# A hybrid decoder layer on one core: each head's first step issued with the output of the head in front, four heads' keys turned by blocks, and lags set per head

## The chip, the cores and the metric

The kernel runs on one core of a Trainium2 chip. The metric is device time in microseconds (us) of one execution; smaller is better. The median of three runs is given, with their lowest and highest.

## What is computed

One layer of a decoder on x of 1024 positions by 1024 channels, all in float32: a token mixer and an MLP, each behind an RMS norm and with a residual, and a last RMS norm.

```python
h = rms_norm(x, norm_mix_g)
u = h @ w_in                                   # 256 pool channels, then q, f, i, g of 6 heads x 128
y_pool = pool_mixer(u_pool, pool_w, pool_scale)
y_hgrn = hgrn2_mixer(q_raw, f_raw, i_raw, g_raw, lb, hgrn_norm_g)
x = x + concat(y_pool, y_hgrn) @ w_out
h2 = rms_norm(x, norm_mlp_g)
x = x + square(relu(h2 @ w_up)) @ w_down       # 4096 wide
return rms_norm(x, final_norm_g)
```

The pool mixer takes means over the last 2, 4, 8 and 16 positions minus the position itself, then a small linear map. Each of the six HGRN heads is a gated linear recurrence with a 128 by 128 state:

```python
S_t = diag(f_t) * S_{t-1} + (1 - f_t) i_t^T    # f = lb + (1 - lb) * sigmoid(z)
o_t = S_t^T q_t
```

followed by an RMS norm per head and a swish gate. It may be computed in chunks of positions: scores within a chunk, and a state handed from chunk to chunk.

## The kernel before

**Dense work.** A dense product in float32 is split in two parts, hi and lo, and made of three matmuls (`mm3`, L129: hi·hi at L132, hi·lo at L133, lo·hi at L134). One such triple is a *step* here. The MLP is dense work alone and the change doesn't touch it.

**Heads.** `hgrn(hd)` (L417) is a generator that makes one head's recurrence out of six stages. Between two stages it stops, and dense work goes on. What stands before a stop is the preparation of the stage that the stop names; what stands behind it are the stage's matmuls, and what follows from them:

- up to "near": the products d0 and d1 and the first `deepen` (three multiplies that work decays into q and k) on VectorE (DVE), and copies `kq` on ScalarE (ACT), L434 and L435;
- "near": column sums (L415) and small matmuls (L443) of neighbouring positions into one bank of PSUM, `sc_near`, which DVE takes into the scores (`take`, L463 and L451); then `deepen` for 2, 4 and 8, with `kq` copies for 4, 8 and 16;
- "middle": matmuls for 4, 8 and 16 into a bank `sc_middle`, taken by DVE as well; `deepen` for 16 and 32;
- "far": scores over 32 and 64 positions; `deepen` for 64;
- "keys": the keys are transposed. Heads 0, 1, 4 and 5 do it on the matmul engine (PE) as `ptk` (L520). Heads 2 and 3 do it *by blocks*: DVE transposes blocks of 32 (L157) and DMAs on SyncE's queue (SP) write them out (L164) and fetch them back in order (L167);
- "updates": what each chunk adds to the state, `pu`: 14 matmuls (L530), or 56 smaller ones (L533) when the keys came by blocks; DVE then adds the states up (`st`);
- "output": the output matmuls `po` (L550, L552), squares on ACT (L555), the reciprocal root on GpSimd (POOL, L141), the scaled output `on` on DVE (L557), and, except for the last head, its transpose by blocks and DMAs.

**What lies beside a head.** `beside(hd)` (L651) gives dense work while head hd runs: q and f of the next head, then a gate. Head 4 has the first pool tile there (`pool_input(0)`). Head 5 has gate 4, then `pool_output(0)`, which is two psp groups of three matmuls (L634), then `pool_input(1)`, 12 steps of gate 5, `pool_output(1)` and the rest. `pool_input` goes from dense matmuls `ps_pool` to `u` (L376), the windowed sums `win` on DVE (L614 to L620), and their split: `whi_win` on ACT (L126), `wlo_win` on DVE (L127). The matmul at psp takes these two.

**What sets the order.** The loop at L770 writes out PE's order by hand: before each stage of head hd it takes so many steps of dense work as `LAGS` says, then goes on with the head's generator. DVE, ACT, POOL and SP get an order from a scheduler, which the tiles' dependences and PE's order shape; each engine then runs its own list in order. `score_ps` has two banks in rotation, used by near, middle, both far ones and by psp; `misc_ps` has three, `dense_ps` three. The decays of a head, `dec`, have a single buffer, as have `Kn` and `S`.

Of the kernel before, what the change touches and what calls it, by code (L numbers as in the profile page):

```python
# [10 lines left out]
F32 = mybir.dt.float32  # L11
# [6 lines left out]
P = 128  # L18
S = 1024
D = 1024  # L20
NT = S // P
# [3 lines left out]
NH = 6  # L25
# [5 lines left out]


STAGES = ("near", "middle", "far", "keys", "updates", "output")
LAGS = {48: (5, 14, 8, 4, 1, 9), 64: (6, 19, 10, 0, 16, 10), 96: (6, 19, 10, 0, 18, 14)}
LAGS = {steps: dict(zip(STAGES, lags)) for steps, lags in LAGS.items()}
FIRST_LAG = 9
WARM_UP = 8
MIX_ORDER = (2, 3, 4, 5, 6, 0, 1, 7)
# [2 lines left out]
TRIO = 3  # L41
# [24 lines left out]
def kernel(  # L66
# [23 lines left out]
    small = ctx.enter_context(tc.tile_pool(name="small", bufs=4))  # L90
# [106 lines left out]
    def mix_tile(n, name):  # L197

        return mixp.tile([P, S], F32, tag="mix" if n < NH - 2 else "late", name=name, bufs=NH - 2 if n < NH - 2 else 2)
# [4 lines left out]
    with ExitStack() as pa:  # L204
# [21 lines left out]
        def queries(t, m):  # L226

            return strided(t, m, [(HALF - m, 2), (2 * m, HALF // (2 * m)), (1, m)])

        def keys(t, m):  # L230
            return strided(t, 0, [(HALF + m, 2), (2 * m, HALF // (2 * m)), (1, m)])

        def sibling(t, of_keys, m):

            n = HALF // m
            off, step = (1, n - 1) if of_keys else (0, n + 1)
            return strided(t, off, [(step, 2), (2, n // 2), (0, m)])
# [28 lines left out]
        vts = {}  # L266
# [63 lines left out]
        def finish(work):  # L330

            while True:
                try:
                    next(work)
                except StopIteration as end:
                    return end.value
# [80 lines left out]
        def hgrn(hd, q, f, k, vt):  # L417
# [10 lines left out]
            dec = ha.tile([P, S], F32, tag="T", name=f"dec_{hd}", bufs=1)  # L428
            t_m, off = deepen(q, k, f, dec, 0, 1)
# [39 lines left out]
            for m in (4, 8, 16):  # L469
                t_m, off = deepen(q, k, t_m, dec, off, m // 2)  # L470
# [10 lines left out]
            t_m, off = deepen(q, k, t_m, dec, off, 16)  # L481
            kq = pairs_of(32)
            t_m, off = deepen(q, k, t_m, dec, off, 32)
# [16 lines left out]
                )  # L500
            act.copy(sc[:64, :4, 64:], ps[:64, :256].rearrange("p (c t) -> p c t", c=4))
            act.copy(sc[64:, 4:, :64], ps[64:, 256:].rearrange("p (c t) -> p c t", c=4))
            t_m, off = deepen(q, k, t_m, dec, off, 64)

            kn = ha.tile([P, NT, P], F32, tag="Kn", name=f"kn_{hd}", bufs=1)
            st = ha.tile([P, NT, P], F32, tag="S", name=f"st_{hd}", bufs=1)
            yield "keys"


            by_blocks = hd in (TRIO - 1, TRIO)  # L510
            if by_blocks:
                turned = ha.tile([P, 4, NT - 1, B], F32, tag="pair", name=f"turned_k_{hd}", bufs=3)
                blocks_turned(turned, k[:, :(NT - 1) * P].rearrange("p (c t) -> p c t", t=P))
# [55 lines left out]
        def deepen(q, k, t_m, dec, off, m):  # L569


            n = S // (2 * m)
            dve.tensor_tensor(out=queries(q, m), in0=queries(q, m), in1=sibling(t_m, False, m), op=ALU.mult)
            dve.tensor_tensor(out=keys(k, m), in0=keys(k, m), in1=sibling(t_m, True, m), op=ALU.mult)
            tv = t_m.rearrange("p (n two) -> p n two", two=2)
            nxt = dec[:, off:off + n]
            dve.tensor_tensor(out=nxt, in0=tv[:, :, 0], in1=tv[:, :, 1], op=ALU.mult)
            return nxt, off + n

        def mixed(hd, on, gate, place=misc_ps):  # L580
            t = mix_tile(hd, f"mix_{2 + hd}")
            mix[2 + hd] = t
            if hd < NH - 1:
                by_quarter = "p (c a i) -> p a c i"
                dve.tensor_tensor(
                    out=t.rearrange(by_quarter, a=4, i=B), in0=on.rearrange("p a (c i) -> p a c i", i=B),
                    in1=gate.rearrange(by_quarter, a=4, i=B), op=ALU.mult,
                )
                return
            for b in range(2):  # L590
                pt = place(f"pto_{hd}_{b}")
                for c in range(4):
                    pe.transpose(pt[:, c * P:(c + 1) * P], on[:, 4 * b + c, :], ident)
                sl = slice(b * 512, (b + 1) * 512)
                dve.tensor_tensor(out=t[:, sl], in0=pt, in1=gate[:, sl], op=ALU.mult)
# [55 lines left out]
        def beside(hd):  # L651

            if hd == TRIO:
                yield from gate(hd - 1)
            if hd + 1 < NH:
                heads[hd + 1] = q, f, k = head_tiles(hd + 1)
                wq = ready_w.pop("q", None) or q_weights(hd + 1)
                for h in range(2):
                    yield from gated(q, wq, h, f"q_{hd + 1}")
                wf = ready_w.pop("f", None) or f_weights(hd + 1)  # L660
                for h in range(2):
                    yield from forget(f, k, wf, h, hd + 1)
            if hd == TRIO - 1:
                yield from dense_V(1)
            elif hd + 2 < NH:
                yield from gate(hd)
            elif hd + 1 < NH:
                pooled[0] = yield from pool_input(0, [mix_tile(NH - 1, f"win{n}_0") for n in range(2)])
            else:
                wins = [ha.tile([P, S], F32, tag=tag, name=f"win{tag}_1", bufs=n) for tag, n in (("K", 2), ("F", 1))]  # L670
                yield from gate(hd - 1)
                pool_output(0, pooled[0])
                pooled[1] = yield from pool_input(1, wins)
                work = gate(hd)
                for _ in range(KT + KT // 2):
                    yield next(work)
                pool_output(1, pooled[1])
                yield from work

        heads, gates, pooled, ready_w, xts, w0 = {}, {}, {}, {}, {}, []  # L680
# [11 lines left out]
        with tc.manual_schedule(engines={mybir.EngineType.PE, mybir.EngineType.DVE, mybir.EngineType.Activation}):  # L692
# [68 lines left out]
            for n in range(2):  # L761
                for e in range(2):
                    nc.sync.dma_start(pw[e * 64:(e + 1) * 64, n, :], pool_w[0, 2 * n + e])
            chain = hgrn(0, *heads[0], vts[0])
            stage = next(chain)
        for e in range(2):
# [3 lines left out]
        with tc.manual_schedule(engines={mybir.EngineType.PE}):  # L770
            for hd in range(NH):
                work = beside(hd)
                lags = LAGS[{TRIO - 1: 96, TRIO: 64}.get(hd, 48)]
                if hd:
                    chain = hgrn(hd, *heads[hd], vts[hd])
                    stage = next(chain)
                while stage:
                    for _ in range(lags[stage] + (FIRST_LAG if hd == 0 and stage == "near" else 0)):
                        next(work, None)
                    if stage == "middle" and hd:  # L780
                        mixed(hd - 1, on, gates[hd - 1])
                    try:
                        stage = next(chain)
                    except StopIteration as end:
                        on, stage = end.value, None
                finish(work)

        def row_block(src, r0, n, c0, name):
# [597 lines left out]
```

## Time and profile before

| | |
|---|---|
| Time, median of three runs | 1065.08 us (1065.07 to 1065.22) |
| Time of the profiled execution | 1065.75 us |
| Its span, first to last instruction | 1063.9 us |
| Mean granted TensorE clock | 0.999 |
| Matmuls on PE | 5960 |
| Instructions in all | 14749 |

The profile is of one execution. What the profiled execution took beyond its span, 1.85 us, lies before the first and after the last instruction. A row of a timeline has the start in the span, the duration, engine, line, operation, output and inputs, and how many instructions went into it; durations of neighbouring rows overlap, since instructions are pipelined, so a cost is the distance from start to start. "128*32" is the part of the array that a matmul uses. A bracket at a row's end is idle time of the engine before it, and what ended it. Lines of the changed kernel are 5 to 8 higher than before's.

### The profile page before, as it was taken

The page shows a single profiled execution, that of the slowest core. Times are in us where ns is not written, and L with a number is a line of the kernel's source. Part 1 is how long each engine was busy: PE and PEld are TensorE (multiplying, and loading weights), DVE is VectorE, ACT ScalarE, POOL GpSimd, SP SyncE. Part 2 cuts the span into 40 slices and gives each one's busy share as a digit, 9 for nine tenths or more (in the row PEclk, how much of TensorE's full clock was granted, in tenths as well). Part 3 has the DMA queues.
Part 4 walks back from the last instruction along what each step waited for, and adds up shares of the span by engine and source line. Part 5 has one row for each costly group of instructions (what it writes and reads, how often), then busy time and mean ns, then how long its engine had stood idle before and what let it go on. Part 6 is the DMA issues. An engine that isn't in the chain of part 4 may idle for free.

```text
span 1063.9 us, 14749 instructions
## 1 busy us (share of the span) xinstructions
PE 1055.2 (99%) x5960; PEld 883.6 (83%) x5960; DVE 750.2 (71%) x934; ACT 444.8 (42%) x716; POOL 77.3 (7%) x126
## 2 busy tenths in 40 slices
PE   9999999999999999999999999999999999999997
PEld 8988888988888888888888888888888888888886
DVE  5377685366688824898855865786979877777775
ACT  5856544344544622563223223322434332424234
POOL 0001010001000111101101100100100000000001
PEclk9999999999999999999999999999999999999999
DMA  9521122132211633135434433528983344253104
GB/s 308 177 61 47 64 71 75 46 96 74 60 41 41 233 135 102 66 102 195 179 100 175 178 118 140 189 108 323 387 318 119 119 160 180 96 209 148 40 1 159
DMA packets 75557, 144.67 MB, mean 136 GB/s; under 512 B 5600, under 2 KB 48352, under 8 KB 71904
## 3 DMA queue, kind: packets, MB, share of 16 engines
q1 hardware_dynamic: 64848, 108.16, 30.0%
q0 software_dynamic: 9344, 33.56, 8.1%
q10 hardware_dynamic: 1296, 2.00, 0.5%
q8 instruction: 47, 0.77, 0.3%
q14 instruction: 22, 0.18, 0.1%
HBM read 102.41 MB, written 41.29 MB: 135 GB/s over the span
## 4 chain that ended last, share of the span: by engine, by line
PE 96%; DVE 2%; issue 1%; DMA 1%; POOL 0%; SPq 0%; ACT 0%; POOLq 0%
PE ps_ua L134 5%; PE ps_ua L133 5%; PE ps_ua L132 5%; PE ps_dx L132 5%; PE ps_dx L133 5%; PE ps_dx L134 5%; PE ps_v L304 3%; PE ps_dy L132 3%; PE ps_uc L134 3%; PE ps_dy L133 3%; PE ps_uc L133 3%; PE ps_dy L134 3%; PE ps_uc L132 3%; PE ps_o L134 3%; PE ps_o L133 3%; PE ps_o L132 2%
## 5 line engine op out<-in xcount | busy, mean ns | idle before, releaser
L126 ACT CAST wdop<-raw_wd 128x2048 fp32r<-128x2048 f32 x28 | 53.6, 1913 | 154.9 <-PE ps_dy L134 49.9
L132 PE MATMUL ps_ua<-h2op,whi_wu 128*128 128x512 f32 x256 | 99.7, 389 | 0.0
L134 PE MATMUL ps_ua<-h2op,wlo_wu 128*128 128x512 f32 x256 | 99.6, 389 | 0.0
L133 PE MATMUL ps_ua<-h2op,whi_wu 128*128 128x512 f32 x256 | 99.6, 389 | 0.0
L132 PE MATMUL ps_dx<-wdop,hop 128*128 128x512 f32 x252 | 98.0, 389 | 0.0
L133 PE MATMUL ps_dx<-wdop,hop 128*128 128x512 f32 x252 | 98.0, 389 | 0.0
L134 PE MATMUL ps_dx<-wdop,hop 128*128 128x512 f32 x252 | 98.0, 389 | 0.0
L127 DVE TENSOR_TENSOR wdop<-raw_wd,wdop 128x2048 fp32r<-128x2048 f32 x28 | 64.1, 2289 | 28.3 <-ACT wdop L126 28.3
L126 ACT CAST hop<-hraw 128x2048 fp32r<-128x2048 f32 x28 | 53.4, 1910 | 32.8 <-DMA hraw<-hid 20.7
L127 DVE TENSOR_TENSOR hop<-hraw,hop 128x2048 fp32r<-128x2048 f32 x28 | 63.9, 2283 | 2.6 <-ACT hop L126 2.6
L126 ACT CAST whi_wu<-wsum 128x1024 fp32r<-128x1024 f32 x22 | 23.2, 1054 | 94.4 <-DVE wsum L845 34.8
L127 DVE TENSOR_TENSOR wlo_wu<-raw_wu,whi_wu 128x1024 fp32r<-128x1024 f32 x23 | 28.0, 1221 | 47.0 <-ACT whi_wu L126 47.0
L848 DVE TENSOR_TENSOR x<-ps_dx,x 128x512 f32<-128x512 f32 x64 | 43.9, 687 | 18.7 <-PE ps_dx L134 18.7
L133 PEld LDWEIGHTS ps_ua<-h2op,whi_wu 128*128 128x128 f32 x256 | 48.1, 188 | 10.0
L132 PEld LDWEIGHTS ps_ua<-h2op,whi_wu 128*128 128x128 f32 x256 | 48.0, 188 | 10.0
L134 PEld LDWEIGHTS ps_ua<-h2op,wlo_wu 128*128 128x128 f32 x256 | 48.0, 188 | 9.9
L134 PEld LDWEIGHTS ps_dx<-wdop,hop 128*128 128x128 f32 x252 | 47.3, 188 | 9.9
L132 PEld LDWEIGHTS ps_dx<-wdop,hop 128*128 128x128 f32 x252 | 47.3, 188 | 9.8
L133 PEld LDWEIGHTS ps_dx<-wdop,hop 128*128 128x128 f32 x252 | 47.3, 188 | 9.7
L1081 POOL DMA_DIRECT2D hid<-hid x56 | 29.8, 532 | 283.6 <-DVE hid L1078 216.5
L132 PE MATMUL ps_uc<-h2op,whi_wu 128*128 128x512 f32 x128 | 49.8, 389 | 0.0
L133 PE MATMUL ps_uc<-h2op,whi_wu 128*128 128x512 f32 x128 | 49.8, 389 | 0.0
(290 smaller groups left out, 2699.3 us busy)
## 6 DMA issues: line engine op xcount, KB each, us to landing
hid<-hid POOLq DMA_DIRECT2D x56, 512.0 KB, 3.2
hraw<-hid SPq DMA_DIRECT2D x28, 1024.0 KB, 5.0
raw_wu<-in_w_up_dram SPq DMA_DIRECT2D x32, 512.0 KB, 3.8
raw_wd<-in_w_down_dram SPq DMA_DIRECT2D x16, 1024.0 KB, 7.1
xt<-in_x_t_dram SPq DMA_DIRECT2D x16, 256.0 KB, 5.6
xn<-in_x_dram SPq DMA_DIRECT2D x8, 512.0 KB, 7.4
x<-x_mid SPq DMA_DIRECT2D x8, 512.0 KB, 5.6
raw_q<-in_w_in_dram SPq DMA_DIRECT2D x6, 512.0 KB, 4.0
```

The source lines that it names most:

```text
L126: act.copy(hi, src)
L127: dve.tensor_tensor(out=lo, in0=src, in1=hi.bitcast(F32), op=ALU.subtract)
L132: pe.matmul(ps, lh, rh, start=start, stop=False, skip_group_check=goes_on)
L133: pe.matmul(ps, lh, rl, start=False, stop=False, skip_group_check=goes_on)
L134: pe.matmul(ps, ll, rh, start=False, stop=stop, skip_group_check=goes_on)
L304: pe.matmul(banks[i][:, :VC], hT[h][part][:, j, i * P:(i + 1) * P], w[:, b, :], start=j == 0 and part == 0 and w is wh, stop=j == KT - 1 a ...
L848: dve.tensor_tensor(out=out_, in0=a, in1=b, op=ALU.add)
L1081: nc.gpsimd.dma_start(store[n][:, at, :], t)
```

## The change

Five things change.

1. `LAGS` is given for each head, instead of for three kinds of heads (by how much dense work there is).
2. Heads 1 to 4 turn their keys by blocks (`TURNED_KEYS`), instead of 2 and 3.
3. The last `deepen`, for 64, writes its decays to a tile of its own, `chunks`, with two buffers, and no longer to the head's `dec`.
4. At the stage "output" of a head, the next head's generator is made and run up to its first stop ahead of the output; behind the output its near stage is issued at once, before the rest of the dense work. Lags for near are 0 from head 1 on.
5. The multiply of a head's output with its gate (`mixed`) is issued before the next head's "far", not before its "middle".

```diff
-LAGS = {48: (5, 14, 8, 4, 1, 9), 64: (6, 19, 10, 0, 16, 10), 96: (6, 19, 10, 0, 18, 14)}
-LAGS = {steps: dict(zip(STAGES, lags)) for steps, lags in LAGS.items()}
+LAGS = (
+    (5, 14, 8, 4, 1, 9), (0, 14, 8, 0, 16, 9), (0, 19, 10, 0, 18, 14), (0, 12, 10, 0, 20, 17), (0, 11, 8, 0, 16, 10),
+    (0, 11, 8, 4, 1, 9),
+)
+LAGS = [dict(zip(STAGES, lags)) for lags in LAGS]
+
+TURNED_KEYS = range(1, NH - 1)
...
-            t_m, off = deepen(q, k, t_m, dec, off, 64)
+            chunks = small.tile([P, NT], F32, tag="chunks", name=f"chunks_{hd}", bufs=2)
+            t_m, _ = deepen(q, k, t_m, chunks, 0, 64)
...
-            by_blocks = hd in (TRIO - 1, TRIO)
+            by_blocks = hd in TURNED_KEYS
...
-                lags = LAGS[{TRIO - 1: 96, TRIO: 64}.get(hd, 48)]
-                if hd:
-                    chain = hgrn(hd, *heads[hd], vts[hd])
-                    stage = next(chain)
+                lags, then = LAGS[hd], None
                 while stage:
                     for _ in range(lags[stage] + (FIRST_LAG if hd == 0 and stage == "near" else 0)):
                         next(work, None)
-                    if stage == "middle" and hd:
+                    if stage == "far" and hd:
                         mixed(hd - 1, on, gates[hd - 1])
+                    if stage == "output" and hd + 1 < NH:
+                        then = hgrn(hd + 1, *heads[hd + 1], vts[hd + 1])
+                        next(then)
                     try:
                         stage = next(chain)
                     except StopIteration as end:
                         on, stage = end.value, None
+                chain = then
+                stage = next(chain) if chain else None
                 finish(work)
```

Three places show what moves. The first is PE at head 5's near matmuls. In before they stand inside the dense work of gate 4 (`ps_g`); L415 and L443 write `sc_near`:

```order
L133 MATMUL ps_g_0_3108<-hT_lo_138,whi_g_2975 128x512
L134 MATMUL ps_g_0_3108<-hT_hi_137,wlo_g_2976 128x512
L415 MATMUL sc_near<-d_5_3092,ones 32x256 x4
L415 MATMUL sc_near<-d_5_3095,ones 32x128 x4
L443 MATMUL sc_near<-kq_2_3102 32x2x16 [waits Activation_49]
L443 MATMUL sc_near<-kq_2_3102 32x2x16 x15
L132 MATMUL ps_g_0_3108<-hT_hi_137,whi_g_2975 128x512
```

In the changed kernel they stand right behind head 4's last output matmuls, `po_1`:

```order
L556 MATMUL po_1_3094<-V_1860,scores 128x128
L558 MATMUL po_1_3094<-st_2909,Q_2356 128x128 [waits DVE_49]
L420 MATMUL sc_near<-d_5_3062,ones 32x256 x4
L420 MATMUL sc_near<-d_5_3065,ones 32x128 x4
L448 MATMUL sc_near<-kq_2_3072 32x2x16 [waits Activation_49]
L448 MATMUL sc_near<-kq_2_3072 32x2x16 x15
L137 MATMUL ps_pool_1_3046<-hT_hi_139,whi_pool_2973 128x512
L138 MATMUL ps_pool_1_3046<-hT_lo_140,whi_pool_2973 128x512
```

So near moved from behind the first pool tile's steps and some steps of gate to the place before the last three steps of the pool tile.

The second place is PE at the two psp groups of `pool_output(0)`, with the gate's last matmul ahead. Before, with the first `sc_middle` of head 5 farther behind:

```order
L134 MATMUL ps_g_1_3181<-hT_hi_139,wlo_g_2976 128x512
L132 MATMUL psp_0_3210<-whi_win_3086,pw_hi 128x512 [waits Activation_49]
L133 MATMUL psp_0_3210<-wlo_win_3087,pw_hi 128x512 [waits DVE_49]
L134 MATMUL psp_0_3210<-whi_win_3086,pw_lo 128x512
L132 MATMUL psp_1_3216<-whi_win_3086,pw_hi 128x512 [waits DVE_49,PE_49,Activation_49]
...
L134 MATMUL ps_pool_0_3235<-hT_hi_137,wlo_pool_3226 128x512 [waits DVE_49]
...
L443 MATMUL sc_middle<-kq_4_3154 32x2x16 [waits PE_49,Activation_49]
```

In the changed kernel `sc_middle` stands ahead, 15 dense matmuls before psp:

```order
L448 MATMUL sc_middle<-kq_4_3152 32x2x16 [waits Activation_49]
...
L139 MATMUL ps_g_1_3222<-hT_hi_139,wlo_g_2980 128x512
L137 MATMUL psp_0_3316<-whi_win_3185,pw_hi 128x512 [waits PE_49,Activation_49]
L138 MATMUL psp_0_3316<-wlo_win_3186,pw_hi 128x512 [waits DVE_49]
L139 MATMUL psp_0_3316<-whi_win_3185,pw_lo 128x512
L137 MATMUL psp_1_3322<-whi_win_3185,pw_hi 128x512 [waits DVE_49,PE_49,Activation_49]
...
L139 MATMUL ps_pool_0_3341<-hT_hi_137,wlo_pool_3332 128x512 [waits DVE_49]
```

The order of banks in `score_ps` is now near, middle, psp, psp, where it was near, psp, psp, middle.

The third place is DVE around the windowed sums `win`: from head 4's last `on` (L557) to the split of the second pool tile's weights, `wlo_pool`. In before the sums follow `u`, with nothing of head 5 between:

```order
L557 TENSOR_TENSOR on_3009<-po_1_3028,rstd_o_1_3044 128x512 [waits Pool_49]
L157 STREAM_TRANSPOSE turned_3047<-on_3009 128x1024 [waits DVE_49,PE_49]
L376 TENSOR_TENSOR u_2966<-ps_pool_1_3005,rms_row 128x4x128 [waits PE_49]
L614 TENSOR_TENSOR win_0_2964<-u_2966 128x1023 [waits DVE_49]
...
L463 COPY_PREDICATED within<-dmask,sc_near 128x256 [waits PE_49]
L573 TENSOR_TENSOR Q_2665<-Q_2665,dec_3097 128x2x64x4 [waits Activation_49]
L127 TENSOR_TENSOR wlo_win_3087<-win_0_2964,whi_win_3086 128x512 [waits Activation_49] x2
...
L127 TENSOR_TENSOR wlo_pool_3226<-raw_pool_3223,whi_pool_3225 128x1024 [waits DMAHW6_49]
```

In the changed kernel, the stretch from the second `on` to the first sum:

```order
L563 TENSOR_TENSOR on_3075<-po_1_3094,rstd_o_1_3110 128x512 [waits Pool_49]
L456 COPY_PREDICATED within<-lmask,sc_near 128x2x32x2 [waits DVE_49]
L162 STREAM_TRANSPOSE turned_3113<-on_3075 128x1024 [waits DVE_49]
L579 TENSOR_TENSOR Q_2732<-Q_2732,dec_3067 128x2x32x8 [waits Activation_49]
L580 TENSOR_TENSOR K_2734<-K_2734,dec_3067 128x2x32x8 [waits Activation_49]
L381 TENSOR_TENSOR u_2970<-ps_pool_1_3046,rms_row 128x4x128 [waits PE_49]
L579 TENSOR_TENSOR Q_2732<-Q_2732,dec_3067 128x2x16x16 [waits Activation_49]
L620 TENSOR_TENSOR win_0_2968<-u_2970 128x1023 [waits DVE_49]
L580 TENSOR_TENSOR K_2734<-K_2734,dec_3067 128x2x16x16 [waits Activation_49]
```

And the one behind the sums, up to `wlo_pool`:

```order
L626 SCALAR_TENSOR_TENSOR win_0_2968<-win_0_2969,pconst,u_2970 64x1024 [waits DVE_49]
L456 COPY_PREDICATED within<-lmask,sc_middle 128x2x16x4 [waits PE_49]
L381 TENSOR_TENSOR g_3193<-ps_g_0_3194,rms_row 128x512 [waits DVE_49]
L132 TENSOR_TENSOR wlo_win_3186<-win_0_2968,whi_win_3185 128x512 [waits Activation_49] x2
L391 SCALAR_TENSOR_TENSOR g_3193<-ps_g_0_3194,hg,g_3193 128x512 [waits Activation_49]
L456 COPY_PREDICATED within<-lmask,sc_middle 128x2x8x8
L579 TENSOR_TENSOR Q_2732<-Q_2732,dec_3067 128x2x8x32
L456 COPY_PREDICATED within<-lmask,sc_middle 128x2x4x16 [waits DVE_49]
L580 TENSOR_TENSOR K_2734<-K_2734,dec_3067 128x2x8x32
L381 TENSOR_TENSOR g_3193<-ps_g_1_3222,rms_row 128x512 [waits PE_49]
L132 TENSOR_TENSOR wlo_pool_3332<-raw_pool_3329,whi_pool_3331 128x1024 [waits Activation_49]
```

With that, four multiplies of head 5's `deepen` and the last take of near stand ahead of the split of `win`, which stood beside or behind it before, and the three takes of `sc_middle` stand among it, ahead of `wlo_pool`.

## The prediction

> **What bounds the kernel now.** I read the page first: its busy shares, then the chain that ended last.
>
> ```profile
> PE 1055.2 (99%) x5960; PEld 883.6 (83%) x5960; DVE 750.2 (71%) x934; ACT 444.8 (42%) x716; POOL 77.3 (7%) x126
> ...
> PEclk9999999999999999999999999999999999999999
> ...
> PE 96%; DVE 2%; issue 1%; DMA 1%; POOL 0%; SPq 0%; ACT 0%; POOLq 0%
> ```
>
> The matmul engine, PE, is busy for 1055.2 of the span's 1063.9 us, and the chain runs along it for 96%. The next view is the list of waits on PE, two rows in all:
>
> ```profile
> PE warm L251 <- DVE junk L249: 1.2, 1, 1.2
> PE ps_v L304 <- DVE wlo_v L127: 0.6, 1, 0.6
> ```
>
> Both lie at the kernel's start. From there on PE never waits for VectorE (DVE), so two things alone can move the time: fewer or shorter PE instructions, and new waits. The kernel's spare time is in the distance between an operand's end and the matmul that takes it, which a busy share doesn't show; for that I read the timelines of PE and DVE side by side at each place where the change moves a matmul nearer to its operand.
>
> **What the change takes from PE.** The timeline of PE around head 1's key transposes:
>
> ```profile
> 129.84 0.93 PE L520 MATMUL ptk<-ident,K 128*128 128x128 f32 x7
> 130.52 0.48 PE L132 MATMUL ps_f<-hT_hi,whi_f 128*128 128x512 f32 x1
> 130.84 0.40 PE L133 MATMUL ps_f<-hT_lo,whi_f 128*128 128x512 f32 x1
> 131.07 0.40 PE L134 MATMUL ps_f<-hT_hi,wlo_f 128*128 128x512 f32 x1
> 131.31 1.72 PE L530 MATMUL pu<-V,kn 128*128 128x128 f32 x14
> 132.78 0.48 PE L132 MATMUL ps_g<-hT_hi,whi_g 128*128 128x512 f32 x1
> ```
>
> Columns: start, duration, engine, line, operation, count. Durations overlap; what counts is start to start. The seven transposes take 0.68 (130.52 − 129.84). The first dense matmul behind them takes 0.32 to the next, where later ones take 0.23 (131.07 − 130.84): a return from small matmuls to dense ones costs 0.09. Heads 1 and 4 lose one such group each: 2 × (0.68 + 0.09) = 1.54 us gained.
>
> Their updates are then made by blocks, as head 2's are now:
>
> ```profile
> 184.00 1.74 PE L533 MATMUL pu<-V,kn 128*32 128x128 f32 x56
> 185.66 0.44 PE L132 MATMUL ps_v<-whi_v,hT_hi 128*128 128x384 f32 x1
> ```
>
> 56 small matmuls take 1.66 where the 14 large ones above took 1.47 (132.78 − 131.31): 2 × 0.19 = 0.38 us lost.
>
> The near matmuls of heads 1 to 5 now stand right behind the output matmuls of the head in front, where dense work parted them before. One return to dense work falls away at each: 5 × 0.09 = 0.45, and as much again if the entry costs what the exit does. I take the lower end, since no row shows two small groups back to back. Where the mixing multiply of a head is issued, at "far" instead of "middle", costs DVE the same and PE nothing. So is the tile that the last product of decays goes to: same size and shape, and its gain, that the next head's decays may be written earlier, only matters where PE waits.
>
> Sum on PE: 1.54 − 0.38 + 0.45 = 1.6 us gained, 1.5 to 2.1, if no wait is added.
>
> **What it adds: head 5.** The early first step needs DVE and ScalarE (ACT) to do head 5's d0, d1 and first deepening before head 4's output is out, and they do. But head 5's second step ("deepen" by 2, 4 and 8, the takes of near, later the takes of middle) now also comes earlier, at lag 11 counted from the output. This is the place where DVE has most to do: it makes the pool mixer's windowed sums, and PE takes them in psp (pool_output(0)). Let P be the time at which head 4's last output matmul gives way. PE needs from there:
>
> ```profile
> 108.40 0.86 PE L415 MATMUL sc_near<-d,ones 128*32 128x256 f32 x16
> ...
> 109.48 0.50 PE L132 MATMUL ps_q<-hT_hi,whi_q 128*128 128x512 f32 x1
> ...
> 119.23 1.06 PE L443 MATMUL sc_middle<-kq 128*32 128x32 f32 x96
> 120.22 0.50 PE L132 MATMUL ps_f<-hT_hi,whi_f 128*128 128x512 f32 x1
> ```
>
> These are head 1's rows, same shapes. Near takes 1.08 and middle 0.99; between them here lie 42 dense matmuls in 9.75, or 0.232 each. Behind P the changed order has near, 42 dense matmuls (3 steps of the first pool tile, and the lag of 11 steps), middle, and 15 dense ones (5 steps of gate) ahead of psp: P + 1.08 + 9.75 + 0.99 + 3.48 = P + 15.3. Now DVE and ACT of before, from P = 301.59 (first row) on:
>
> ```profile
> 301.59 0.48 PE L132 MATMUL ps_pool<-hT_hi,whi_pool 128*128 128x512 f32 x1
> ...
> 318.68 0.39 PE L132 MATMUL psp<-whi_win,pw_hi 128*128 128x512 f32 x1
> ...
> 320.55 0.39 PE L134 MATMUL ps_pool<-hT_hi,wlo_pool 128*128 128x512 f32 x1
> ```
>
> ```profile
> 305.64 0.69 DVE L557 TENSOR_TENSOR on<-po,rstd_o 128x512 f32<-128x512 f32 x1 [1.12 <-POOL rstd_o L141]
> 306.43 1.25 DVE L157 STREAM_TRANSPOSE turned<-on 128x1024 f32<-128x1024 f32 x1
> 307.60 0.65 DVE L376 TENSOR_TENSOR u<-ps_pool,rms_row 128x512 f32<-128x512 f32 x1
> 308.29 1.23 DVE L614 TENSOR_TENSOR win<-u 128x1023 f32<-128x1023 f32 x1
> ...
> 313.90 0.45 DVE L463 COPY_PREDICATED within<-dmask,sc_near 128x256 f32<-128x256 uint8 x1
> 314.25 0.68 DVE L573 TENSOR_TENSOR Q<-Q,dec 128x512 f32<-128x512 f32 x1
> 314.84 1.29 DVE L127 TENSOR_TENSOR wlo_win<-win,whi_win 128x512 fp32r<-128x512 f32 x2
> 316.05 0.45 DVE L451 COPY_PREDICATED within<-lmask,sc_near 128x128 f32<-128x128 uint8 x1
> 316.27 0.73 DVE L574 TENSOR_TENSOR K<-K,dec 128x512 f32<-128x512 f32 x1
> ...
> 318.99 1.22 DVE L127 TENSOR_TENSOR wlo_pool<-raw_pool,whi_pool 128x1024 fp32r<-128x1024 f32 x1
> 320.13 0.74 DVE L386 SCALAR_TENSOR_TENSOR g<-ps_g,hg,g 128x512 f32<-128x512 f32 x1
> ```
>
> ```profile
> 310.68 0.62 ACT L434 COPY kq<-Q 128x512 f32<-128x512 f32 x1 [7.18 <-PE sc_near L415]
> 311.21 0.62 ACT L435 COPY kq<-K 128x512 f32<-128x512 f32 x1
> ...
> 313.90 1.15 ACT L126 CAST whi_win<-win 128x512 fp32r<-128x512 f32 x2 [2.08 <-DVE win L620]
> ```
>
> Before, psp starts at P + 17.1, and its operands are in time: wlo_win ends at 316.13. The second psp needs a free bank of the two that the scores share, so near must have been taken; that too was so, since middle stood behind psp. wlo_pool, at 320.21, is 0.34 ahead of its matmul at 320.55.
>
> Prices from these rows, start to start: a 512-column multiply 0.60 (314.25 to 314.84), a take 0.22 (316.05 to 316.27), the transpose 1.17, u 0.69, a half of wlo_win 0.60, wlo_pool 1.14, the chain of sums 5.61 (308.29 to 313.90), a half of whi_win 0.57 (1.15 / 2).
>
> Changed, DVE's order by the program is: second `on`, take, transpose, Q, K, u, Q, chain of sums with one K inside, take, g, wlo_win twice, g, take, Q, take, K, g, wlo_pool. The second `on` began at P + 4.05. Two kq copies on ACT, 0.53 each (310.68 to 311.21), now get between the squares that it needs; I add 0.8, so P + 4.85.
> - `on`, take, transpose, Q, K, u, Q: 0.60 + 0.22 + 1.17 + 0.60 + 0.60 + 0.69 + 0.60 = 4.48. The chain starts at P + 9.3, where before it started at P + 6.7.
> - 5.61 + 0.60: done at P + 15.5. First half of whi_win on ACT: P + 16.1.
> - take, g, half of wlo_win: P + 16.9; second half 17.5.
> - g, take, Q, take: 0.60 + 0.22 + 0.60 + 0.22: P + 19.2. Only now are the last scores of middle out of their bank, and the second psp needs that bank, since near, middle, psp, psp follow each other through two.
> - K, g, wlo_pool: 2.34: P + 21.5.
>
> And PE: psp could start at 15.3, starts at 16.1 (wait 0.8); its second matmul could at 16.3, starts at 16.9 (0.6); the second psp could at 17.4, starts at 19.2 (1.8); three rows of it and two of ps_pool later, 20.3, the wlo_pool matmul starts at 21.5 (1.2). Together 4.4 us. DVE has no gap in this stretch, so the bounds come from its start: if the squares aren't interrupted, 0.8 less; if every multiply takes its full duration (0.68 instead of 0.60, 10 of them), 0.8 more. So 3.6 to 5.2 us lost.
>
> The other places look easier. For the second pool column tile's psp in the same head and the outputs of head 1, where lags are short too, I allow nothing to 0.6 us and take 0.2: an allowance, not a reading.
>
> **Two rules weighed.** By the rows above the stall comes in pieces of 0.8, 0.6, 1.8 and 1.2 with matmuls between them, and the granted clock of before is 9 tenths or more in all 40 slices. The one place where the trace shows PE coming out of idleness is its start:
>
> ```profile
> L251 PE MATMUL warm<-junk 128*128 128x512 bf16 x8 | 3.6, 631 | 1.2 <-DVE junk L249 1.2
> ```
>
> Eight matmuls of 512 columns have 3.6 us of busy time there; dense ones at 0.232 would need 1.9. So a fall of the clock is worth about 1.7 us once. The Trainium skill, page "TensorE: Matmul & The Clock Gate", section "HAM oscillation — how this bites in real kernels", says "no PE-idle gaps >~3.4µs": by it the clock would stay, as the largest piece is 1.8, and the sum is unchanged; were the pieces taken as one gap of 4.4, its rule would add the price just named. No run so far shows a gap of this kind.
>
> **The rivals.**
> 1. *VectorE's backlog stays hidden; not slower.* If the chain of sums kept its old place, P + 6.7, and ran without Q, K between, every operand would be at least 2.6 us earlier, and the bank wait would vanish if middle's takes came before them. Then only the 1.6 stays: 1065.1 − 1.6 = 1063.5. For it: DVE is busy 71% over the span. Against it: DVE goes in program order, and there is no gap in 305.64 to 320.13 to take up 5 us. It decides where the backlog is under 0.8 us. A milder form, half the backlog met (2 us), gives 1065.4.
> 2. *The clock falls.* The pieces act as one gap: 1.7 on top, 1069.8.
> 3. *Keys by blocks land late.* Head 2's go out and back by DMA today:
>
> ```profile
> 176.84 0.34 SPq L164 DMA_DIRECT2D k<-turned_k  x1
> 179.96 1.79 SPq L167 DMA_DIRECT2D kn<-k  x4
> ```
>
> The first is issued at 176.84 and PE's updates start at 184.00: 7.2 us later. Heads 1 and 4 now do the same with 16 dense steps (48 × 0.232 = 11.1 us) between, which holds it; heads 2 and 3 keep 18 and 20. In SP's queue the returns stand behind weight loads, which can hold them. A late landing of 1 us somewhere gives 1069.0.
>
> That the change doesn't do what it says is no rival: the order of PE shows near behind the output and the transposes gone.
>
> **How the numbers follow.** The profiled run took 1065.75, 0.67 above the median of the three runs, 1065.08; a difference is carried over to the median. Forecast: 1065.08 − 1.6 + 4.4 + 0.2 = 1068.1, with its own range of −2.1 + 3.6 + 0 to −1.5 + 5.2 + 0.6, or 1066.6 to 1069.4. A measurement of this kernel can tell 0.2% from no change, 2.13 us: same is 1062.95 to 1067.21.
>
> Chances: forecast 0.64; rival 1 0.12, its milder form 0.10; rival 2 0.06; rival 3 0.08. Slower by more than 2.13: nine tenths of the forecast (0.58), rivals 2 and 3: 0.72. Same: the rest of the forecast (0.06), the milder form and three quarters of rival 1: 0.25. Faster: a quarter of rival 1, where the entries also count: 0.03. The range leaves out rival 1 and little beyond rival 2's price: 1064.3 to 1070.2.
>
> **What would show it.** Right: PE has waits of 0.6 to 2 us at psp and the ps_pool behind it, in head 5 only, released by DVE and ACT, some 4.4 us around 316 to 323 of the span; transposes ptk come 14 times, not 28, updates by blocks 224 times; near starts right behind po; DVE has no gap from the second `on` to wlo_pool; the granted clock stays at 9. Wrong on the stall: psp without a wait; wrong on its parts: the wait before the second psp not released by a take of sc_middle; wrong on PE's gain: span less waits more than 0.5 us off 1063.9 − 1.6. A wait at the updates (L539) or a digit under 9 would speak for rivals 3 or 2.

## The result, and the profile after

The changed kernel takes 1080.64 us (median of 4 runs, 1080.33 to 1081.99), where before takes 1065.07: ratio 1.015, interval 1.0137 to 1.0163. It is slower, as forecast, but by 15.6 us, where 3.0 were forecast and 5.1 was the end of the range. The profiled execution took 1081.99, its span is 1080.2 us, 16.3 more than before's.

The page has PE busy for 12.7 us more, which no wait explains, and one slice of the clock under 9:

```profile
PE 1067.9 (99%) x6030; PEld 884.0 (82%) x6030; DVE 751.5 (70%) x936; ACT 443.6 (41%) x712; POOL 78.0 (7%) x126
...
PEclk9999999999998999999999999999999999999999
```

The waits on PE behind the start are at the places that the prediction named, and one at the updates. Columns: total, how often, the longest:

```profile
PE psp L137 <- DVE within L456: 1.6, 1, 1.6
...
PE psp L138 <- DVE wlo_win L132: 1.1, 2, 0.7
PE ps_pool L139 <- DVE wlo_pool L132: 0.8, 1, 0.8
PE pu L539 <- DMA kn<-k: 0.4, 1, 0.4
PE psp L137 <- ACT whi_win L131: 0.3, 1, 0.3
```

PE's timeline there. A bracket is idle time behind the modelled end of the matmul in front, so the loss is a little more: the distance from start to start, less 0.23.

```profile
317.93 0.39 PE L139 MATMUL ps_g<-hT_hi,wlo_g 128*128 128x512 f32 x1
318.61 0.49 PE L137 MATMUL psp<-whi_win,pw_hi 128*128 128x512 f32 x1 [0.29 <-ACT whi_win L131]
319.48 0.50 PE L138 MATMUL psp<-wlo_win,pw_hi 128*128 128x512 f32 x1 [0.37 <-DVE wlo_win L132]
319.81 0.39 PE L139 MATMUL psp<-whi_win,pw_lo 128*128 128x512 f32 x1
321.83 0.47 PE L137 MATMUL psp<-whi_win,pw_hi 128*128 128x512 f32 x1 [1.63 <-DVE within L456]
...
322.84 0.40 PE L138 MATMUL ps_pool<-hT_lo,whi_pool 128*128 128x512 f32 x1
324.07 0.80 PE L139 MATMUL ps_pool<-hT_hi,wlo_pool 128*128 128x512 f32 x1 [0.83 <-DVE wlo_pool L132]
324.66 0.63 PE L137 MATMUL ps_pool<-hT_hi,whi_pool 128*128 128x512 f32 x1
```

Losses: 0.45, 0.64, 1.79 and 1.00, together 3.9 us, where 0.8, 0.6, 1.8 and 1.2 were forecast. The last row has 0.63 where a dense matmul has 0.39: the clock has fallen. The trace records when the granted clock changes: here it falls to half at 323.40 and comes back at 330.23. Three stretches around that show it. Columns: the stretch, its length, the busy time of PE, PEld (the weight loads), DVE, ACT and POOL, each with its number of instructions, then the granted clock, the DMA share and GB/s:

```profile
319.99:323.40 3.41, 1.61 (x6) 0.86 (x5) 3.41 (x8) 3.38 (x8) 0.00 (x0) 1.00 0.00 0
323.40:326.82 3.42, 2.75 (x7) 2.16 (x7) 3.02 (x4) 1.80 (x4) 0.00 (x0) 0.50 0.41 121
326.82:330.23 3.41, 3.41 (x36) 2.62 (x35) 1.47 (x3) 1.65 (x6) 0.00 (x0) 0.50 0.62 189
```

The clock is at half for 6.8 us, which loses 3.4, some of it while PE waits anyway. Stall and clock are 7 us. The rest is nowhere near head 5. Here is a stretch of the MLP, far behind all that the change moves, first of before, then of the changed kernel; PE's busy time comes with the number of its matmuls:

```profile
500.00:600.00 100.00, 100.00 (x443) 82.81 (x442) 71.38 (x73) 28.41 (x37) 9.04 (x17) 1.00 0.42 148
```

```profile
500.00:600.00 100.00, 100.00 (x437) 81.54 (x436) 67.36 (x67) 32.25 (x41) 7.46 (x14) 1.00 0.39 139
```

437 matmuls where 443 were, with the clock at 1.00 and PE never idle: each takes longer from start to start. Where it begins, the timeline of the changed kernel shows a step from one row to the next:

```profile
398.57 0.39 PE L139 MATMUL ps_o<-whi_wo,mT_lo 128*128 128x512 f32 x1
...
401.97 0.39 PE L139 MATMUL ps_o<-whi_wo,mT_lo 128*128 128x512 f32 x1
402.19 0.39 PE L137 MATMUL ps_o<-wo,mT_hi 128*128 128x512 f32 x1
...
407.79 0.39 PE L137 MATMUL ps_o<-wo,mT_hi 128*128 128x512 f32 x1
```

Fifteen matmuls from 398.57 to 401.97 take 0.2267 each; from 402.19, where the moving operand comes from another tile (`wo` instead of `whi_wo`; rows name it ahead of the weights), 24 take 0.2333 each. The duration column says 0.39 for both; only the distance of the starts shows it.

What differs between these tiles is their place. The new tile `chunks` has two buffers of 32 bytes per partition, in a pool that stands ahead of most others. Where the built programs put tiles (bytes within a partition):

```
pool (a tile of it)        before   changed
big    (hT_hi, mT, hop)     24032     24096   64 higher
wsplit (whi_, wlo_)         89568     89632   64 higher
hraw   (hop)               122336    122400   64 higher
big2   (wo, h2op)          180192    180192   not moved: from the other end
```

In before, the moving operand and the weights of every dense matmul but twelve (psp) start at addresses that agree modulo 256. In the changed kernel, of 4032 there are 1236 with the moving operand in a pool that stayed and weights in one that moved, and 480 the other way round. I took the distance of the starts over all neighbouring rows of the trace with the same pair of places: 0.2270 in before (3828 pairs); in the changed kernel 0.2274 where they agree (2141 pairs), 0.2334 (1192) and 0.2312 (472) where they don't. That would be 1236 × 0.0066 + 480 × 0.0044 = 10.3 us. Why the chip takes longer for such a pair, no run here shows; the runs show the price.

### The profile page after: what moved, and what is told of

Its sections match the earlier page's. It is cut to its first block, busy times and chain, and to the rows that moved or that the text cites. A ratio compares the mean times of both kernels' runs of the same rounds, so it can differ in the third digit from the quotient of the medians.

```text
span 1080.2 us, 14893 instructions
## 1 busy us (share of the span) xinstructions
PE 1067.9 (99%) x6030; PEld 884.0 (82%) x6030; DVE 751.5 (70%) x936; ACT 443.6 (41%) x712; POOL 78.0 (7%) x126
## 4 chain that ended last, share of the span: by engine, by line
PE 95%; DVE 3%; DMA 1%; POOL 0%; issue 0%; ACT 0%; SPq 0%; POOLq 0%
PE ps_ua L138 5%; PE ps_ua L137 5%; PE ps_ua L139 5%; PE ps_dx L137 5%; PE ps_dx L138 5%; PE ps_dx L139 5%; PE ps_v L309 3%; PE ps_dy L138 3%; PE ps_dy L139 3%; PE ps_dy L137 3%; PE ps_o L137 3%; PE ps_o L139 3%; PE ps_uc L139 3%; PE ps_uc L138 3%; PE ps_uc L137 3%; PE ps_o L138 3%
## 5 line engine op out<-in xcount | busy, mean ns | idle before, releaser
L137 PEld LDWEIGHTS ps_dx<-wdop,hop 128*128 128x128 f32 x252 | 47.3, 188 | 10.8
L139 PEld LDWEIGHTS ps_dx<-wdop,hop 128*128 128x128 f32 x252 | 47.3, 188 | 10.8
L137 PE MATMUL ps_dy<-wdop,hop 128*128 128x512 f32 x128 | 50.7, 396 | 0.0
L138 PE MATMUL ps_dy<-wdop,hop 128*128 128x512 f32 x128 | 50.7, 396 | 0.0
L139 PE MATMUL ps_dy<-wdop,hop 128*128 128x512 f32 x128 | 50.7, 396 | 0.0
```

What stands on the lines that cost most here:

```text
L137: pe.matmul(ps, lh, rh, start=start, stop=False, skip_group_check=goes_on)
L138: pe.matmul(ps, lh, rl, start=False, stop=False, skip_group_check=goes_on)
L139: pe.matmul(ps, ll, rh, start=False, stop=stop, skip_group_check=goes_on)
```

## The experiments

**Is it the addresses? Four shifts and one return.** The theory: dense matmuls are slower where their two operands' addresses disagree. The rival, called aftermath below: the MLP's slow pitch (the distance of the starts) is left over from the stall and the clock. The first kernel is before with 64 bytes more in one constant tile; no engine's order changes.

```diff
-    nhalf = const.tile([P, NT], F32, name="nhalf")
+    nhalf = const.tile([P, NT + 16], F32, name="nhalf")
```

> The kernel before, with 64 bytes added to one constant tile and nothing else; every tile of the pools on the left of the memory lies 64 bytes higher, as the tile chunks does it in the changed kernel, those on the right stay. Theory (addresses): in the changed kernel 1236 dense matmuls whose moving operand and weights start at addresses that differ by 64 modulo 128 took 0.2334 us from start to start, and 480 of the other sign 0.2312, where 0.227 stands for those that agree; so 1236 x 0.0066 + 480 x 0.0044 = 10.3 us slower, 1075.4. Rival (aftermath): the slow pitch of the MLP is left over from the stall and the clock's fall in head 5, which this kernel doesn't have; 1065.1.

Measured: 1075.76 us against 1065.29, ratio 1.010 (1.0083 to 1.0117). The addresses alone cost 10.5 us. The stretch of its MLP:

```profile
500.00:600.00 100.00, 100.00 (x436) 81.54 (x436) 70.25 (x72) 28.97 (x37) 8.50 (x16) 1.00 0.41 143
```

The same line in the changed kernel should have put things right, I thought, since 64 and 64 are 128:

> The changed kernel with 64 bytes added to the same constant tile: with the 64 of chunks, everything on the left lies 128 bytes higher than before, and operands agree modulo 128 again. Theory (addresses): 10.3 us less than the changed kernel's 1080.6, so 1070.3, with the waits at psp (some 4.2 us) and the half clock behind them (some 3.4 us) still there, and the dense pitch of the MLP 0.227. Rival (aftermath): 1080.6, pitch 0.230.

Measured: 1080.93, no gain, and 437 matmuls in the stretch of 100 us:

```profile
500.00:600.00 100.00, 100.00 (x437) 81.76 (x436) 68.62 (x69) 31.25 (x40) 7.44 (x14) 1.00 0.40 139
```

So the theory with 128 fell: pairs that differ by 128 took 0.2330 (1192) and 0.2328 (472). It could be 256 or 512, as operands agree modulo 512 in before. `NT + 64`, 256 bytes, tells these apart:

> The kernel before with 256 bytes added to one constant tile. 1716 dense matmuls then have operands whose starts differ by 256 modulo 512, 0 modulo 256. If the modulus is 256: 1065.1, pitch 0.227. If it is 512 (they agree modulo 512 before, and not modulo 1024): about 1716 x 0.006 = 10 us slower, 1075.

Measured: 1065.24, ratio 1.0001 (0.999 to 1.0011), and before's count again:

```profile
500.00:600.00 100.00, 100.00 (x443) 82.81 (x442) 71.34 (x73) 28.33 (x37) 9.03 (x17) 1.00 0.42 148
```

So 256 bytes cost nothing: the modulus is 256. And the smallest step that I tried, `NT + 8`, 32 bytes:

> The kernel before with 32 bytes added to one constant tile: 1236 and 480 dense matmuls have operands that differ by 32 modulo 256. Theory (any difference modulo 256 costs 0.006 us): about 10 us slower, 1075. Rival (only a difference of 64 or more costs, since 32 bytes is half of what the others moved): 1065.1, or part of the 10 us.

Measured: 1076.62 (2 runs) against 1064.59, ratio 1.0111 (1.0093 to 1.0129); 0.2333 in both kinds of pairs. There is no milder price for this smaller difference. Against the 0.2270 of before, 1716 × 0.0063 is 10.8 of the 12.0 us in the medians; the spans of the two profiled executions are 11.0 apart (1074.9 and 1063.9).

Last, the changed kernel without the shift: 64 bytes are saved at a tile that needs no four buffers.

```diff
-        warm = small.tile([P, 1], F32, tag="ss", name="warm")
+        warm = small.tile([P, 1], F32, tag="ss", name="warm", bufs=2)
```

> The changed kernel with nothing moved in memory: one small tile, warm, gets two buffers instead of four (64 bytes less), so that with the 64 of chunks every tile lies where it lay before; every engine's order is the changed kernel's. Theory (addresses, as it stands after the shift by 128: what counts is whether moving operand and weights agree modulo 256 or 512): the MLP's pitch is 0.227 again, 10.3 us less, so 1080.6 - 10.3 = 1070.3, with the stall (4.2) and the half clock behind it (3.4) in it. Rival: the pitch is not a matter of addresses in this kernel, since the shift by 128 left 1080.9: 1080.6.

Measured: 1070.44 against 1065.11, ratio 1.005 (1.0035 to 1.0065): 10.2 us of the 15.6 were the place of `chunks`. Left are 5.3 us, 0.2 over the upper end of what the prediction had thought the whole could cost, with the half clock in them. That lasted 3.4 us here, from 322.11 to 325.52, where it had lasted 6.8:

```profile
318.70:322.11 3.41, 1.40 (x4) 0.69 (x5) 3.41 (x8) 3.41 (x6) 0.00 (x0) 1.00 0.00 0
322.11:325.52 3.41, 3.41 (x8) 2.18 (x8) 3.02 (x5) 3.08 (x8) 0.00 (x0) 0.50 0.07 12
```

**Is the stall head 5's early step?** The changed kernel with head 5's first step behind head 4's dense work, and its old lags:

```diff
-    (0, 11, 8, 4, 1, 9),
+    (5, 14, 8, 4, 1, 9),
...
-                    if stage == "output" and hd + 1 < NH:
+                    if stage == "output" and hd + 2 < NH:
...
                 finish(work)
+                if hd + 2 == NH:
+                    chain = hgrn(hd + 1, *heads[hd + 1], vts[hd + 1])
+                    stage = next(chain)
```

> The changed kernel, but head 5's first step is made after head 4's dense work, with the lags that it had before (5, 14, 8, 4, 1, 9), so that middle stands behind psp again; heads 1 to 4 stay as changed, and chunks too. Theory (addresses): the waits at psp and the fall of the clock go, 4.2 + 3.4 us, the slow pitch of the MLP stays: 1073.0. Rival (aftermath): with the stall gone the pitch of the MLP is 0.227 again, and all is gone: 1063.6.

Measured: 1076.80, ratio 1.0111 (1.0096 to 1.0126): 3.8 us less than the changed kernel, where 7.6 were expected. The waits at psp are gone and the clock stays at 9, but a wait came in their place:

```profile
PE ps_pool L139 <- DVE wlo_pool L132: 1.6, 1, 1.6
...
PE pu L539 <- DMA kn<-k: 0.2, 1, 0.2
```

Head 4's lags grew by four steps in the change, so psp and the second pool tile stand 19 steps behind head 4's output where they stood 23: the sums on DVE still start from that output. I had taken the whole distance for head 5's. With the shift by 128 beside it, which was meant to mend the addresses and doesn't:

> Both mended: head 5's first step late as before, and the 64 bytes added that make operands agree modulo 128. Theory (addresses) and rival (aftermath) alike: what is left is the gain on the matmul engine that the prediction worked out, 1.6 us less one re-entry of 0.1: 1063.6. A third theory, that the changed order of heads 1 to 4 loses elsewhere by waits (keys by blocks landed 0.4 us late once in the changed kernel's profile): 1064.0 to 1065.

Measured: 1076.63, as without it (ratio 1.0108, 1.0093 to 1.0123). Both are the address term, the wait for wlo_pool (1.8 from start to start), the 0.2 at the updates and the gain, worked out further down as 1.2: 10.2 + 1.8 + 0.2 − 1.2 = 11.0, where 11.5 and 11.3 were measured.

**Is the second psp's wait for middle's bank?** The changed kernel, addresses as before, and middle behind psp:

```diff
-    (0, 11, 8, 4, 1, 9),
+    (0, 17, 8, 4, 1, 9),
```

> The changed kernel with nothing moved in memory, as above, and head 5's lag ahead of middle 17 instead of 11: middle stands behind psp, so that the second psp's bank is free once near is taken. Theory of the prediction (the wait of 1.6 at the second psp is for the bank that middle holds): that piece goes; psp and wlo_pool's matmul come nearer to their operands by middle's 1.0 us, so about 3.5 to 4 us of stall in three pieces. Theory (the clock falls by the sum of pieces within a few us, not by one gap over 3.4): the clock may fall again, 1070. Rival (one gap must be longer than 3.4): the clock stays at 9 and the time is 1067.5. If the bank is not the cause, the wait at the second psp is still released by a take.

Measured: 1068.67 against 1065.11, ratio 1.0035 (1.0023 to 1.0048), 1.8 us better than with 11. The wait that a take released is gone, as the prediction's bank said; the first psp waits longer instead, since PE is there sooner:

```profile
PE psp L137 <- ACT whi_win L131: 1.5, 1, 1.5
...
PE ps_pool L139 <- DVE wlo_pool L132: 1.0, 1, 1.0
PE psp L138 <- DVE wlo_win L132: 0.4, 2, 0.2
```

The clock stayed, and the time is 1.2 above the 1067.5 expected for that. Three pieces are left:

```profile
317.18 0.39 PE L139 MATMUL ps_g<-hT_hi,wlo_g 128*128 128x512 f32 x1
319.06 0.50 PE L137 MATMUL psp<-whi_win,pw_hi 128*128 128x512 f32 x1 [1.49 <-ACT whi_win L131]
319.81 0.50 PE L138 MATMUL psp<-wlo_win,pw_hi 128*128 128x512 f32 x1 [0.24 <-DVE wlo_win L132]
...
321.40 0.40 PE L138 MATMUL ps_pool<-hT_lo,whi_pool 128*128 128x512 f32 x1
322.80 0.50 PE L139 MATMUL ps_pool<-hT_hi,wlo_pool 128*128 128x512 f32 x1 [1.01 <-DVE wlo_pool L132]
```

From start to start, less 0.23 each, that is 1.65, 0.52 and 1.17: 3.3 us in all.

**What is the change worth without shift and stall?** Two kernels give psp its 23 steps back, with head 5 late and nothing moved in memory. One leaves head 4's keys on PE:

```diff
-TURNED_KEYS = range(1, NH - 1)
+TURNED_KEYS = range(1, NH - 2)
...
-(0, 11, 8, 0, 16, 10),
+(0, 19, 8, 4, 1, 9),
```

> Nothing moved in memory; near of heads 1 to 4 directly behind the output in front, head 5 as before (5, 14, 8, 4, 1, 9), head 4's keys on the matmul engine as before with lags (0, 19, 8, 4, 1, 9), so that psp stands as far behind head 4's output as before; keys by blocks for heads 1 to 3. Theory (the terms of the prediction without stall): one group of transposes gone, 0.77, updates by blocks 0.19 more, four returns to dense work 4 x 0.09: 0.94 gained, 1064.1 where before has 1065.1; no wait on the matmul engine behind the start. Rival (a wait comes up elsewhere): 1065 or more.

Measured: 1066.78 against 1064.67, ratio 1.0022 (1.0013 to 1.0032): the rival. psp doesn't wait, but behind the heads a new wait stands, by the profile for head 5's scaled output, ahead of the second step of the output product. Neither before nor the next kernels have it. What ties the two is open: in the last kernel below, `on` starts no earlier (352.70, here 352.63), and no output product waits for it.

```profile
PE ps_o L137 <- DVE on L563: 2.4, 1, 2.4
```

The other takes the four steps from head 4's middle and far:

```diff
-(0, 11, 8, 0, 16, 10),
+(0, 9, 6, 0, 16, 10),
```

> Nothing moved in memory; heads 1 to 4 as in the changed kernel but head 4's lags (0, 9, 6, 0, 16, 10), four steps shorter, so that psp stands as far behind head 4's output as before; head 5 as before. Theory: two groups of transposes gone, 1.54, updates 0.38 more, four returns 0.36: 1.5 gained, 1063.6. Rival (head 4's middle or far matmuls now wait for VectorE, since four steps are 2.8 us less for the same work): 1064 to 1066, with waits at L448 or L502.

Measured: 1064.03 against 1064.67, ratio 0.9993 (0.9984 to 1.0002). The gain is 0.6, less than half of the 1.5. The list of waits has one of 0.3 us at head 2's updates for the keys' DMA, and none at L448 or L502; but PE's timeline has 0.80 from the first of head 4's far scores at L448 (275.86) to the first at L502 (276.66), where before has 0.52, so the rival's place costs 0.3 too. Two more steps ahead of head 2's updates:

```diff
-(0, 19, 10, 0, 18, 14)
+(0, 19, 10, 0, 20, 14)
```

> The kernel with head 5 late, head 4 four steps shorter and nothing moved in memory, and head 2's lag ahead of the updates 20 steps instead of 18, so that its keys have landed: the wait of 0.3 us at the updates goes. Theory: 1.5 us under before by the prediction's terms with no wait, 1063.4 to 1063.6 where before has 1064.7 to 1065.1. Rival (what is gained is half of that, as the kernel with lag 18 measured 0.64): 1064.0.

Measured: 1063.67 against 1064.59, ratio 0.9991 (0.9982 to 1.0). All waits on PE lie within the start now:

```profile
PE warm L256 <- DVE junk L254: 1.2, 1, 1.2
PE ps_v L309 <- DVE wlo_v L132: 0.6, 1, 0.6
PE ps_v L309 <- ACT whi_v L131: 0.3, 1, 0.3
```

It is the lowest of all, 0.9 us under before, with an interval that just reaches no change. Expected was 1.5; 0.9 is nearer to the rival's 0.6.

## Why the prediction was wrong, point by point

**The step that failed.** "So is the tile that the last product of decays goes to: same size and shape, and its gain ... only matters where PE waits." I costed `chunks` as an instruction with another output, at nothing, and did not cost its 64 bytes. They move every pool behind them, and not those allocated from the other end, and with that the addresses of operands of 1716 matmuls that the change never mentions. It was 10.2 us of 15.6 (changed kernel with and without the shift), 10.5 put into before by itself. Nothing in the page of before shows it, as all its dense matmuls agree but the twelve of psp, which are too few to see there. On PE's timeline of before, the six of them ahead of the second pool tile take 0.2333 each (318.68 to 320.08), the price that disagreeing pairs pay in the changed kernel.

**The stall was right, place by place.** In the changed kernel head 4's output gives way to near at P = 302.81, by PE's timeline; DVE's follows:

```profile
302.81 0.86 PE L420 MATMUL sc_near<-d,ones 128*32 128x256 f32 x16
```

```profile
307.46 0.69 DVE L563 TENSOR_TENSOR on<-po,rstd_o 128x512 f32<-128x512 f32 x1 [0.78 <-POOL rstd_o L146]
...
311.84 1.22 DVE L620 TENSOR_TENSOR win<-u 128x1023 f32<-128x1023 f32 x1
...
317.93 0.30 DVE L456 COPY_PREDICATED within<-lmask,sc_middle 128x128 f32<-128x128 uint8 x1
...
321.40 0.29 DVE L456 COPY_PREDICATED within<-lmask,sc_middle 128x128 f32<-128x128 uint8 x1
...
322.80 1.22 DVE L132 TENSOR_TENSOR wlo_pool<-raw_pool,whi_pool 128x1024 fp32r<-128x1024 f32 x1
```

The second `on` starts at P + 4.65 (forecast 4.85), the sums at P + 9.0 (9.3), they are done at P + 15.1 (15.5); psp starts at P + 15.8 (16.1), its second matmul at P + 16.7 (16.9), the second psp at P + 19.0 (19.2), the wlo_pool matmul at P + 21.3 (21.5). The whole is 3.9 us, within 3.6 to 5.2. That the second psp waits for middle's bank, the kernel with middle behind psp showed.

**The small allowance** of 0.2 for other places was too low. PE's timeline at the second pool tile's psp:

```profile
352.64 0.40 PE L137 MATMUL psp<-whi_win,pw_hi 128*128 128x512 f32 x1
353.74 0.50 PE L138 MATMUL psp<-wlo_win,pw_hi 128*128 128x512 f32 x1 [0.70 <-DVE wlo_win L132]
```

That is 0.9 us (1.10 less 0.23), and head 2's updates lost 0.4 to their keys' DMA: rival 3 had its cause right, with 0.4 instead of 1.

**The clock, rival 2,** had 0.06 and came true, but not because the pieces act as one gap. Its price of 1.7 is what the kernel without the shift shows (3.4 us at half); in the changed kernel's profile it was twice that. The sentence of the Trainium skill that I had set beside it, page "TensorE: Matmul & The Clock Gate", section "HAM oscillation — how this bites in real kernels", asks for "no PE-idle gaps >~3.4µs". By it the clock would have stayed; it fell with no gap longer than 1.64. The sum of the pieces doesn't decide either. Without the shift the clock fell at 322.11, when 0.44, 0.64 and 1.79, together 2.9 us, had been lost from start to start; with middle behind psp it stayed with 3.3.

What fits every profiled execution is PE's busy share in one stretch of 3.41 us. The changes of the clock lie whole multiples of 3.413 us apart. In the changed kernel, without the shift and with the shift by 128, the clock first rises at 5.96, 4.67 and 7.11, falls 317.44 us later (93 times 3.413), and comes back after 6.83, 3.41 and 3.41. With stretches of that length laid from the first rise, PE is busy for 1.61, 1.40 and 1.57 us of the one that ends with the fall, less than half of it. The emptiest ones of kernels that kept the clock have 1.78 and 1.77 (head 5 late, without and with the shift by 128), 1.95 (middle behind psp) and 1.97 (keys of heads 1 to 3 by blocks). First head 5 late, then middle behind psp:

```profile
317.77:321.18 3.41, 1.78 (x8) 1.16 (x7) 3.41 (x6) 3.41 (x7) 0.00 (x0) 1.00 0.00 0
```

```profile
315.62:319.03 3.41, 1.95 (x9) 1.29 (x7) 3.24 (x4) 0.64 (x2) 0.00 (x0) 1.00 0.09 30
```

In the changed kernel the wait for wlo_pool reached into the first stretch at half, with 2.75 of 3.42 busy, and the clock came back only behind the next, full one; in the other two the first was full. By this reading it also matters where the stretches happen to lie, so that one kernel can keep its clock in one execution and lose it in another. The times look so: with the shift by 128 one execution took 1079.61 at a mean clock of 0.998, the other three 1080.84 to 1081.18 at 0.996 or 0.997; with keys by blocks for heads 1 to 3, three of ten took 1068.1 to 1068.3 at 0.997, the others 1066.4 to 1067.0 at 0.998 or 0.999. The reading was made from the traces afterwards; no run was made to test it, and where between 1.61 and 1.77 of 3.41 it turns is open.

**The gain of 1.6** was 0.4 too high, below its range of 1.5 to 2.1. From the first matmul of `ps_q` to the first of `ps_o`, PE takes 311.39 us in before and 310.45 in the best kernel, 0.94 less, and the medians say 0.9. (The spans differ by 1.5, but 0.4 of that lies ahead of the first `ps_q`, which starts at 40.26 and 39.89.) The keys cost what was forecast: 0.68 per group of transposes, and 0.38 more for the updates. What failed is the 0.45 for returns to dense work. The changed kernel has the two small groups back to back that before didn't have; first before's output giving way to dense work, then the changed kernel's giving way to near:

```profile
301.45 0.39 PE L552 MATMUL po<-st,Q 128*128 128x128 f32 x2
301.59 0.48 PE L132 MATMUL ps_pool<-hT_hi,whi_pool 128*128 128x512 f32 x1
```

```profile
302.49 0.39 PE L558 MATMUL po<-st,Q 128*128 128x128 f32 x2
302.81 0.86 PE L420 MATMUL sc_near<-d,ones 128*32 128x256 f32 x16
```

The last two output matmuls take 0.14 in front of dense work and 0.32 in front of near: 0.18 more. What falls away is the return, 0.09, and as much at near's other side, where before's dense matmul ahead of near takes 0.32 to the next start. So joining the two groups gained nothing, and 1.54 − 0.38 = 1.2 is left; the best kernel loses another 0.3 of it in head 4's far scores. By the sum: 10.2 for the addresses, 3.9 and 0.9 and 0.4 for the waits, 1 to 2 for the clock beyond them, less 1.2, is the 15.6 to within 0.6; runs of the changed kernel differ by 1.7 among themselves, about what 3.4 us more or less at half clock make.

**Rival 1** (hidden backlog) is ruled out by DVE's timeline: the chain of sums starts at P + 9.0, not at P + 6.7, and behind the second `on` DVE has no gap up to wlo_pool that could take a backlog up.

## What to carry to other kernels

A new tile is costed by where it pushes its neighbours, too: compare the operands' addresses in the built program modulo 256 before and after, above all where pools are allocated from two ends. When a dense stretch that a change doesn't touch gets slower with PE busy and the clock full, count matmuls per 100 us and look at the distance of starts; durations don't show it. Whether a stall costs the clock as well was told here neither by its longest piece nor by their sum, but by PE's busy time in one stretch of 3.41 us. And the distance from a producer to its consumer is counted in steps between the two in program order, wherever the steps were taken away: here four of them had gone from the head in front.

## What the runs showed of the hardware that was not expected

- A dense matmul of 512 columns takes 0.227 us from start to start where the starts of its moving operand and of its weights agree modulo 256 bytes, and 0.231 to 0.233 where they differ by 32, 64, 128, 192 or 224; other differences weren't tried. By 256 it is 0.2267 again. With 1716 of 4032 of them disagreeing, the kernel is 1.0% slower.
- Short idle pieces can cost the clock. It fell to 0.50 where PE had been busy for 1.40, 1.57 or 1.61 us of one stretch of 3.41 us, with no gap over 1.64, and stayed at 1.00 where it had been busy for 1.77 to 1.97. The stretches lie in steps of 3.413 us from the clock's first rise, and it came back at the end of one in which PE had been busy throughout.
- From start to start, the matmul behind an idle piece takes 0.31 to 0.34 to the next (319.48 to 319.81 in the changed kernel), as one does that returns from small matmuls: each wait costs some 0.1 beyond its length.
- A group of small matmuls right behind another isn't free: the last 128x128 output matmul takes 0.205 to the start of a 128*32 one, and 0.03 to that of a dense one.
